# Band attention with split scores: the second score product over 128 contraction rows instead of 64

## The chip, the core and the metric

The kernel runs on one core of one Trainium2 chip. The metric is device time in microseconds (us) of one execution. Below, PE is the matrix engine (TensorE), PEld its weight loads, DVE the vector engine, ACT the scalar engine, POOL GpSimd and SP the engine that issues most DMAs.

## What is computed

One layer of a hybrid trunk on 1024 tokens of width 1024: a normalised input is projected once to q, k, v, gates and a state-space input; a band attention and a state-space mixer run on it; both are gated, merged, projected back, added to the input and normalised. Only the attention is touched here. It has 8 heads of 64 channels; a chunk of 64 queries sees its own chunk of keys and the 8 before it, with a bias by relative position:

```
scores = jnp.einsum("bnqhd,bnkhd->bnhqk", qc, k_band,
                    preferred_element_type=jnp.float32) * ATTN_SCALE
...
scores = jnp.where(valid, scores + bias[None, None], NEG_INF)
probs = jax.nn.softmax(scores, axis=-1).astype(v.dtype)
out = jnp.einsum("bnhqk,bnkhd->bnqhd", probs, v_band)
```

## The kernel before

**Split products.** Every matrix product is made from operands split in two parts: a high part rounded to the reduced type that PE reads (F32R), and a low part, the remainder. A projection adds three products into one PSUM bank (`mm3`, L104 to L106): high by high, high by low, low by high. The low by low part is left out.

**Scores.** A head has only 64 channels, so the 128 rows of the array are shared by two parts of a head. For head e of a pair, `qq` holds the high part of q twice (rows 0 to 63 and 64 to 127), `k2` holds the high part of k on the head's own rows (0 to 63 for the first head of a pair, 64 to 127 for the second) and the low part of k on the other rows. One product over 128 rows (L910) gives q high by k high plus q high by k low. The third term, q low by k high, is a second product over the 64 own rows only (L911); `ql` is one tile that holds the low q of both heads, each on its own rows. Both products accumulate into the same tile `s`.

**Where these come from.** `evac_q` (L690 to L704) runs once per half of the tokens and per pair of heads. It reads the projection's bank `mm` and for each head makes two ACT copies into `qq` (L702, the own rows; L703, the other rows) and one DVE subtraction into `ql` (L704; the trace records it under the helper's line L92). `evac_k` (L706) does the same for `k2`, with one ACT copy and one DVE subtraction per head.

**Order of the attention.** Heads are taken one after the other, query tiles of 128 in pairs. `scores` (L895) takes one query tile: with up to four key tiles it is one chunk of up to 512 columns, with five it is two chunks of 320. For each chunk PE runs L910 and L911, then DVE adds the bias and takes the row maximum (L912). ACT takes the exponential (L919), DVE a reciprocal (L920), POOL scales (L921). Two pairs of query tiles later (`LAG`), PE turns the probabilities (`turn`, L939), ACT and DVE split the turned tile into `th` and `tl` (L98, L101), and PE multiplies them with v (`prod`, L957 and L958) into `pv`, of which there is a single bank. When half of a head's queries is done, ACT and DVE add the two halves of `pv` to `y` (L964 and L965; DVE's part is recorded under L83), which frees that bank.

PE's order is written out by hand: `drive` interleaves the attention's steps with the pieces of projections (three products of 512 columns each): q and k of the next pair of heads during the first three pairs, gate columns during the last. The program's planner chooses the order on the other engines. Tile `s` has two PSUM banks (`ps_2`), the projections three (`ps_m`), the turned blocks two (`ps_t`).

The score products run from 244 to 472 us of the profile's span. The first pair's q is made before that stage, those of the other three pairs inside it.

Of the kernel before, what the change touches and what calls it, by code (L numbers as in the profile page):

```python
# [9 lines left out]
F32 = mybir.dt.float32  # L10
# [7 lines left out]
P = 128  # L18
L = 1024          # tokens
D = 1024          # model width  # L20
KT = D // P       # 8 k-tiles of the model width
HALF = 512
NH = 8
DH = 64
GC = 16           # channels of a state-space group
NS = 64           # states of a group
T8 = 8            # tokens of a state-space chunk
NJ = L // T8      # 128 chunks
NP = 16           # pairs of groups
MAGIC = 12582912.0  # L30
ET = mybir.EngineType
RATE_SSM = 1.0                              # steps of the state-space mixer per piece of a projection
SSM_STEPS = [8, 4, 4, 0, 2, 28, 20, 4]      # steps between its stages
RATE_ATT = 1.012                            # steps of the attention, relative to an even spread
PATTERN = "STSTT"                           # scores, and turns with products, in a step of the attention
LAG = 2                                     # pairs of query tiles between scores and products
NU = 4                                      # tiles of v from x * gain, scaled afterwards
NPM = 3                                     # psum banks of the projections
NPB = 7                                     # probability tiles
NGA = 5                                     # tiles of g_a during the third pair of heads  # L40
NWARM = 20
CUTS = [0, 512, 768, 1024]                  # column blocks of the last tile
# [3 lines left out]
def trunk_kernel(ctx: ExitStack, tc: tile.TileContext, x, x_t, ng, w_m, w_v, bias, a_re, a_im, log_dt,  # L46
# [26 lines left out]
    # the tensor engine's clock rises while the first loads are under way  # L73
# [34 lines left out]
    def rsqrt(pool_, v, out=None):  # L108
        """1 / sqrt(v), a few columns at a time: a root and a Newton step."""
        w = v.shape[1]  # L110
        r = pool_.tile([P, 4], F32, tag="rs_r", name="rs_r")[:, :w]
        u = pool_.tile([P, 4], F32, tag="rs_u", name="rs_u")[:, :w]
        vec.reciprocal(out=u, in_=v)
        last_sqrt[0] = act.activation(out=r, in_=u, func=AF.Sqrt)
        if w == 1:
            stt(u, r, v, r, MUL, MUL)
        else:
            tt(u, r, r, MUL)
            tt(u, u, v, MUL)
        ts(u, u, -0.5, MUL, 1.5, ADD)  # L120
        o = r if out is None else out
        tt(o, r, u, MUL)
        return o

    def rsqrt_mean(pool_, ss, n, eps, out=None):
        """1 / sqrt(ss / n + eps)"""
        v = pool_.tile([P, 4], F32, tag="rs_v", name="rs_v")[:, :ss.shape[1]]
        ts(v, ss, 1.0 / n, MUL, eps, ADD)
        return rsqrt(pool_, v, out)

# [1 line left out]
    # A task: (dma, split, run, number of yields of run). The weights of a task are loaded while  # L132
    # the one before it starts, and split into exact high and low parts in its middle.
# [14 lines left out]
    class Stream:  # L148
# [7 lines left out]
        def run(self, tasks, after=None):  # L156
            """Yields between pieces of the matrix products."""
            for n, (_, _, run, ny) in enumerate(tasks):
                nxt = tasks[n + 1] if n + 1 < len(tasks) else after
                w, raw = self.w, None  # L160
                if nxt is not None:
                    with tc.high_priority():
                        raw = nxt[0]()
                for i, _ in enumerate(run(w)):
                    if i == max(ny // 2 - 1, 0) and nxt is not None:
                        with tc.high_priority():
                            self.w = nxt[1](raw)
                    yield

    stream = Stream()  # L170
    hT = []           # [hi 0-3, hi 4-7], [lo 0-3, lo 4-7]

    def proj(w, half):
        """A projection tile: 128 columns of w_in on partitions, 512 tokens."""
        wh, wl = w
        ps = pm()
        sl = slice(half * HALF, (half + 1) * HALF)
        for k in range(KT):
            q, r = divmod(k, 4)
            mm3(ps, wh[:, k, :], wl[:, k, :], hT[0][q][:, r, sl], hT[1][q][:, r, sl], k == 0, k == KT - 1)  # L180
            if k < KT - 1:
                yield None
        yield ps

    def proj_task(src, evac):
        """evac(half, psum) takes the products of a half of the tokens."""
# [8 lines left out]
    def drive(main, back, rate):  # L195
        """Runs the generator main, and about rate steps of back for each of its steps."""
        acc = 0.0
        for _ in main:
            acc += rate() if callable(rate) else rate
            while acc >= 1.0:  # L200
                next(back, None)
                acc -= 1.0

# [1 line left out]
    sp = {}  # L205

    def ssm_params(tp, cpool):
# [63 lines left out]
        # cos and sin: quarter turns taken off exactly, then polynomials  # L271
# [38 lines left out]
        # powers of the discrete eigenvalue  # L310
# [9 lines left out]
        # B of the discrete system  # L320
# [18 lines left out]
        # |lambda|^8 and the unit phase to the 8th, then its powers of two  # L339
# [6 lines left out]
        def sqr(orr, oi, ar, ai):  # L346
# [4 lines left out]
            # the norm stays 1  # L351
# [13 lines left out]
        # D on the diagonal of the first tap  # L365
# [16 lines left out]
    def ssm_batch(b, sb, u_ready):  # L382
# [23 lines left out]
        # E: state at the end of a chunk from the chunk's inputs (rows: tap, channel)  # L406
# [6 lines left out]
        # Q: outputs from a state, by the age of the state (0..8)  # L413
# [40 lines left out]
        # powers of the chunk's phase  # L454
# [27 lines left out]
        # taps within a chunk, with D on the first, spread to a block Toeplitz matrix  # L482
# [34 lines left out]
    def load_x(i):  # L517
        """A tile of 128 tokens, for the mean squares."""
# [6 lines left out]
    def load_xt(i, whole=True):  # L525
        """The tile turned, for h^T."""
# [39 lines left out]
    def root(tiles):  # L566
        """One over the root mean square of each token."""
# [8 lines left out]
    def bcast(tiles):  # L576
        """The same on every partition."""
# [20 lines left out]
    def scale(i, q, bc):  # L598
        """h^T of a tile, a half of its rows."""
# [16 lines left out]
    def head(i, q):  # L616
        """x * gain, split."""
# [17 lines left out]
    def v_evac(ps, i):  # L635
        """The first tiles are products of x * gain, and take the mean squares here."""
# [19 lines left out]
    def u_task(b):  # L656
        box = {}

        def evac(half, ps):
# [3 lines left out]
            # the taps of a chunk in falling order  # L663
# [22 lines left out]
    def qk_tasks(p):  # L686
        """Heads 2p and 2p+1: [q;q] high, low q of both, [k high;k low] (second head: [low;high])."""
        hs = pairs[p] = [{}, {}]

        def evac_q(half, ps):  # L690
# [7 lines left out]
            sl = slice(half * HALF, (half + 1) * HALF)  # L698
            for e in range(2):
                own, oth = slice(64 * e, 64 * e + 64), slice(64 - 64 * e, 128 - 64 * e)  # L700
                qq, ql = hs[e]["qq"], hs[e]["ql"]
                act.activation(out=qq[own, sl], in_=ps[own], func=AF.Copy, scale=0.125)  # L702
                act.activation(out=qq[oth, sl], in_=ps[own], func=AF.Copy, scale=0.125)  # L703
                stt(ql[own, sl], ps[own], 0.125, qq[own, sl].bitcast(F32), MUL, SUB)  # L704
# [79 lines left out]
    def before(i, k):  # L784
        """What is emitted before product k of tile i."""
# [109 lines left out]
    def scores(h, i, bt, probs):  # L895
        """Exponentials of the scores of 128 queries, and one over their sums on a diagonal."""
        hd = pairs[h // 2][h % 2]
        e = h % 2
        own = slice(64 * e, 64 * e + 64)
# [7 lines left out]
        for c in range(nb):  # L907
# [3 lines left out]
            pe.matmul(ps, hd["ql"][own, qsl], hd["k2"][own, ksl], start=False, stop=True)  # L911
# [14 lines left out]
    class Values:  # L926
        """Probabilities turned, up to four blocks of 128 x 128 at a time, and multiplied by V."""
# [40 lines left out]
    # sigmoid(g_a) of the first tiles goes where the q and k of the pairs before were  # L968
# [19 lines left out]
    def turns(i):  # L988
        """The key tiles of the query tiles i and i + 1, in groups of at most four blocks."""
# [7 lines left out]
    def attention():  # L997
        """Pairs of query tiles; PATTERN: the order of scores, turns and products in a step."""
# [199 lines left out]
    with tc.tile_pool(name="fin", reuse_waits="tile", bufs=2) as fin:  # L1198
        fg_b = fin.tile([P, D], F32, name="fg_b", bufs=1)
        nc.scalar.dma_start(out=fg_b, in_=fg.partition_broadcast(P))  # L1200
        for i in range(KT):
# [13 lines left out]
            def add_x(n, ps):  # L1215
                """The row with x, its mean square so far, and the row times the gain."""
# [35 lines left out]
def _layout(inp):  # L1252
# [6 lines left out]
    wt = mt(w_in)                       # 40 tiles of 128 columns  # L1259
    # within a tile of the state-space channels: channel of a group first, then group  # L1260
# [4 lines left out]
             + list(range(24, 40)))     # u, z_a, q and k by head pairs, z_s, g_a, g_s  # L1265
# [48 lines left out]
```

## Time and profile before

| | |
|---|---|
| median of 3 runs | 837.65 us (837.37 to 838.12) |
| span of the profiled execution, first to last instruction | 836.3 us |
| PE busy over the span | 825.2 us (99%) |
| DVE busy | 480.9 us (58%) |
| ACT busy | 371.2 us (44%) |
| score products L910 and L911 | 96 each |

Of the profiled execution the page gives the span; the median of the runs is 1.35 us longer, which is what lies before the first and behind the last instruction, give or take the scatter of the runs.

How to read it: in a timeline row the first number is the start in us from the span's beginning, the second the duration. Matmuls are pipelined and the ends of their rows are modelled, so durations of neighbours overlap. What a matmul costs the stream is the distance from its start to the next start. PEld rows are weight loads: each matmul has one, and it can run beside the matmul before it. "idle before <-issue" on a PEld row is time in which the loading side stood still without any wait that the profile can name. `64*128` in a row is a weight tile of 64 rows.

### The profile page before, as it was taken

Reading aid. Unit: us, or ns where it says so; the run is one execution under the profiler, and the core shown is the slowest. Engines: PE = TensorE matmul, PEld = TensorE weight load, DVE = VectorE, ACT = ScalarE, POOL = GpSimd, SP = SyncE. Lnnn points to the kernel's source line nnn. Section 1 sums busy time; section 2 is a strip of 40 time slices with the busy share of each in tenths; the row PEclk is TensorE's granted clock in tenths of the full one; section 3 lists DMA queues with packets and bytes.
Section 4 is the critical chain, followed back from the end, with each engine's and each line's share of the span. In section 5 each row is a group of like instructions: output and inputs, shape, how many; then the busy total and the mean of one; then the engine's idle time right before and its main releaser. Section 6 shows DMA issues by size and latency. Waiting matters only on the chain.

```text
span 836.3 us, 11001 instructions
## 1 busy us (share of the span) xinstructions
PE 825.2 (99%) x3942; PEld 667.2 (80%) x3942; DVE 480.9 (58%) x1326; ACT 371.2 (44%) x701; POOL 127.2 (15%) x171
## 2 busy tenths in 40 slices
PE   8999999999999999999999999999999999999996
PEld 6878888888877777777777788888888888888885
DVE  6899898886646676676544532335353332354442
ACT  5652565645546456565443565116242211324332
POOL 4450022011003223323221200000000000001110
PEclk9999999999999999999999999999999999999999
DMA  8604352223330001110101044114113110042221
GB/s 310 246 26 125 91 137 69 100 81 119 112 107 31 23 31 42 42 42 1 42 26 51 26 141 136 62 41 150 51 51 114 41 62 13 6 145 101 101 101 51
DMA packets 32455, 67.84 MB, mean 81 GB/s; under 512 B 4560, under 2 KB 13776, under 8 KB 32400
## 3 DMA queue, kind: packets, MB, share of 16 engines
q1 hardware_dynamic: 27904, 61.35, 21.6%
q10 hardware_dynamic: 3344, 3.42, 1.4%
q0 software_dynamic: 1152, 2.36, 1.3%
q8 instruction: 31, 0.51, 0.2%
q14 instruction: 24, 0.20, 0.1%
HBM read 56.14 MB, written 10.98 MB: 80 GB/s over the span
## 4 chain that ended last, share of the span: by engine, by line
PE 96%; DVE 2%; DMA 1%; issue 0%; ACT 0%; SPq 0%; POOL 0%; ACTq 0%; POOLq 0%
PE mm L104 27%; PE mm L106 25%; PE mm L105 25%; PE s L911 4%; PE pt L939 3%; PE s L910 2%; PE pv L958 2%; PE pv L957 2%; PE pt L442 1%; PE b L468 1%; PE pt L503 1%; PE pt L504 1%; DMA xt<-in_x_t_dram 1%; DVE xt L601 0%; PE pt L426 0%
## 5 line engine op out<-in xcount | busy, mean ns | idle before, releaser
L104 PE MATMUL mm<-hT,w_hi 128*128 128x512 f32 x576 | 237.6, 413 | 0.0
L106 PE MATMUL mm<-hT,w_lo 128*128 128x512 f32 x576 | 225.7, 392 | 0.7 <-DVE w_lo L101 0.7
L105 PE MATMUL mm<-hT,w_hi 128*128 128x512 f32 x576 | 225.5, 392 | 0.0
L106 PEld LDWEIGHTS mm<-hT,w_lo 128*128 128x128 f32 x576 | 108.2, 188 | 24.3 <-DVE w_lo L101 1.2
L104 PEld LDWEIGHTS mm<-hT,w_hi 128*128 128x128 f32 x576 | 108.4, 188 | 23.2 <-issue 6.7
L105 PEld LDWEIGHTS mm<-hT,w_hi 128*128 128x128 f32 x576 | 108.7, 189 | 16.1 <-issue 0.4
L101 DVE TENSOR_TENSOR w_lo<-w_raw,w_hi 128x1024 fp32r<-128x1024 f32 x36 | 44.0, 1223 | 66.1 <-ACT w_hi L98 65.9
L912 DVE CUSTOM_DVE_ANT_0 p<-s,bias 128x320 f32<-128x320 f32 (+2 forms) x96 | 46.6, 490 | 34.0 <-PE s L911 31.7
L98 ACT ACTIVATE w_hi<-w_raw 128x1024 fp32r<-128x1024 f32 x36 | 38.1, 1059 | 62.9 <-PE mm L105 52.9
L101 DVE TENSOR_TENSOR tl<-pt,th 128x512 fp32r<-128x512 f32 (+2 forms) x72 | 43.2, 601 | 38.1 <-ACT th L98 37.6
L98 ACT ACTIVATE th<-pt 128x512 fp32r<-128x512 f32 (+2 forms) x72 | 37.8, 525 | 59.9 <-PE pt L939 54.0
L921 POOL TENSOR_SCALAR p<-p,sm 128x640 f32<-128x640 f32 (+2 forms) x64 | 42.5, 665 | 139.2 <-DVE sm L920 109.0
L919 ACT ACTIVATE p<-p,mx 128x640 f32<-128x640 f32 (+2 forms) x64 | 44.3, 692 | 38.3 <-DVE mx L89 18.2
L83 POOL TENSOR_TENSOR x<-x,fg_b 128x512 f32<-128x512 f32 (+1 forms) x9 | 11.0, 1225 | 319.0 <-ACT o L1219 319.0
L104 PE MATMUL mm<-y_hi,o_hi 128*128 128x512 f32 x128 | 49.8, 389 | 0.0
L105 PE MATMUL mm<-y_lo,o_hi 128*128 128x512 f32 x128 | 49.8, 389 | 0.0
L106 PE MATMUL mm<-y_hi,o_lo 128*128 128x512 f32 x128 | 49.8, 389 | 0.0
L98 ACT ACTIVATE o_hi<-o_raw 128x512 fp32r<-128x512 f32 x24 | 15.0, 631 | 71.7 <-PE mm L105 60.3
L911 PE MATMUL s<-k,ql 64*128 64x320 f32 (+2 forms) x96 | 39.3, 409 | 0.0
L939 PE MATMUL pt<-ident,p 128*128 128x128 f32 x240 | 38.9, 276 | 0.0
L957 PE MATMUL pv<-th,vt 128*128 128x256 f32 x144 | 36.0, 272 | 0.2
L939 PEld LDWEIGHTS pt<-ident,p 128*128 128x128 f32 x240 | 28.9, 140 | 9.0 <-issue 1.9
(231 smaller groups left out, 1512.8 us busy)
## 6 DMA issues: line engine op xcount, KB each, us to landing
w_raw<-in_w_m_dram SPq DMA_DIRECT2D x36, 512.0 KB, 3.3
x<-in_x_dram SPq DMA_DIRECT2D x16, 512.0 KB, 6.3
wo_raw<-in_w_out_dram SPq DMA_DIRECT2D x8, 512.0 KB, 3.2
xt<-in_x_t_dram SPq DMA_DIRECT2D x6, 512.0 KB, 9.7
bias<-in_bias_dram SPq DMA_DIRECT2D x8, 320.0 KB, 2.8
wv_raw<-in_w_v_dram SPq DMA_DIRECT2D x8, 256.0 KB, 5.6
u_dr<-us SPq DMA_DIRECT2D x4, 512.0 KB, 3.6
uu<-u_dr SPq DMA_DIRECT2D x4, 512.0 KB, 3.8
```

Of the source, the lines that this page charges most:

```text
L98: act.activation(out=hi, in_=src, func=AF.Copy)
L101: (eng or vec).tensor_tensor(out=lo, in0=src, in1=hi.bitcast(F32), op=SUB)
L104: pe.matmul(ps, lh, rh, start=first, stop=False)
L105: pe.matmul(ps, lh, rl, start=False, stop=False)
L106: pe.matmul(ps, ll, rh, start=False, stop=last)
L910: pe.matmul(ps, hd["qq"][:, qsl], hd["k2"][:, ksl], start=True, stop=False)
L911: pe.matmul(ps, hd["ql"][own, qsl], hd["k2"][own, ksl], start=False, stop=True)
L912: vec.tensor_tensor_reduce(out=pr[:, c * cw:(c + 1) * cw], in0=ps, in1=bt[:, 640 - w + c * cw:640 - w + (c + 1) * cw], scale=1.0, scalar=- ...
L919: act.activation(out=pr[:, :w], in_=pr[:, :w], func=AF.Exp, bias=mx[:, 0:1], accum_out=sm)
L921: pool.tensor_scalar(out=pr[:, :w], in0=pr[:, :w], scalar1=sm, scalar2=1.0, op0=MUL, op1=MUL)
L939: last_turn[0] = pe.transpose(tp[:, n:n + P], probs[h, q][:, k * P:(k + 1) * P], ident).ins
L957: pe.matmul(o, lhs, th[:, cs], start=first and n == 0, stop=False)
```

## The change

Two edits.

In `scores`, the second product runs over all 128 rows of `ql` and `k2`. On the own rows it gives low q by high k as before. On the other rows it now multiplies the other head's low q by this head's low k, which is not wanted.

In `evac_q`, that extra term is taken off in advance: the copy of `qq` on the other rows, which meets the low k in the first product, is no longer the high part of q but q (scaled) minus the other head's low q. What is added in the second product cancels in the first. The ACT copy L703 becomes a DVE operation of the same shape, and it has to wait for the other head's `ql`.

```
     def evac_q(half, ps):
...
             sl = slice(half * HALF, (half + 1) * HALF)
+            own = [slice(64 * e, 64 * e + 64) for e in range(2)]
+            ql = hs[0]["ql"]
             for e in range(2):
-                own, oth = slice(64 * e, 64 * e + 64), slice(64 - 64 * e, 128 - 64 * e)
-                qq, ql = hs[e]["qq"], hs[e]["ql"]
-                act.activation(out=qq[own, sl], in_=ps[own], func=AF.Copy, scale=0.125)
-                act.activation(out=qq[oth, sl], in_=ps[own], func=AF.Copy, scale=0.125)
-                stt(ql[own, sl], ps[own], 0.125, qq[own, sl].bitcast(F32), MUL, SUB)
+                qq = hs[e]["qq"]
+                act.activation(out=qq[own[e], sl], in_=ps[own[e]], func=AF.Copy, scale=0.125)
+                stt(ql[own[e], sl], ps[own[e]], 0.125, qq[own[e], sl].bitcast(F32), MUL, SUB)
+            for e in range(2):
+                oth = own[1 - e]
+                stt(hs[e]["qq"][oth, sl], ps[own[e]], 0.125, ql[oth, sl].bitcast(F32), MUL, SUB)
...
     def scores(h, i, bt, probs):
         hd = pairs[h // 2][h % 2]
-        e = h % 2
-        own = slice(64 * e, 64 * e + 64)
...
             pe.matmul(ps, hd["qq"][:, qsl], hd["k2"][:, ksl], start=True, stop=False)
-            pe.matmul(ps, hd["ql"][own, qsl], hd["k2"][own, ksl], start=False, stop=True)
+            pe.matmul(ps, hd["ql"][:, qsl], hd["k2"][:, ksl], start=False, stop=True)
```

The rest of the diff removes comments. Numbers and order of the instructions on PE stay the same.

## The prediction

> **What bounds the kernel now.** I read the page first: busy times, then the chain that ended last.
>
> ```profile
> span 836.3 us, 11001 instructions
> ...
> PE 825.2 (99%) x3942; PEld 667.2 (80%) x3942; DVE 480.9 (58%) x1326; ACT 371.2 (44%) x701; POOL 127.2 (15%) x171
> ...
> PE 96%; DVE 2%; DMA 1%; issue 0%; ACT 0%; SPq 0%; POOL 0%; ACTq 0%; POOLq 0%
> ```
>
> The matrix engine is the bound nearly everywhere: what is taken from PE's stream comes off the end, as long as nobody else becomes late. But "busy" only says that a matmul was under way. So next the busy time by stretches, for the stage of the score products and for what follows it. The columns are the stretch, its length, the busy time (and instructions) of PE, PEld, DVE, ACT and POOL, the granted clock, the DMA share and GB/s:
>
> ```profile
> 244.00:472.00 228.00, 227.76 (x1139) 170.78 (x1137) 140.57 (x430) 124.36 (x261) 61.32 (x89) 1.00 0.10 33
> 472.00:836.00 364.00, 356.96 (x1623) 296.88 (x1622) 143.96 (x273) 120.89 (x231) 14.41 (x12) 1.00 0.24 80
> ```
>
> In the 228 us of the stage PE has 0.2 us without a matmul, DVE is at 62%, ACT at 55%, and the clock is full. Third, the view of the tile `s`, whose row for L911 gives the number of second products and their widths (the 8 that are missing from its list are 512 wide):
>
> ```profile
> L911 PE MATMUL s<-k,ql x96: 323/410/502, 244.5 to 472.0; 64*128 64x320 f32 x64, 64*128 64x128 f32 x8, 64*128 64x256 f32 x8, 64*128 64x384 f32 x8
> ```
>
> Fourth, PE's timeline, in which I read distances from start to start. A tile with one chunk of 512 columns, then the three products of a projection:
>
> ```profile
> 302.34 0.45 PE L910 MATMUL s<-k,qq 128*128 128x512 f32 x1
> 302.71 0.49 PE L911 MATMUL s<-k,ql 64*128 64x512 f32 x1
> 303.14 0.50 PE L104 MATMUL mm<-hT,w_hi 128*128 128x512 f32 x1
> 303.48 0.40 PE L105 MATMUL mm<-hT,w_hi 128*128 128x512 f32 x1
> 303.71 0.39 PE L106 MATMUL mm<-hT,w_lo 128*128 128x512 f32 x1
> ```
>
> All five stream 512 columns. L105 to L106, full rows behind full rows, takes 0.23 us. L911 takes 0.43, L910 ahead of it 0.37, and L104 behind it 0.34. So the short product costs more than a full one, and its neighbours on both sides pay too. The weight loads of the same moment show why:
>
> ```profile
> 302.71 0.18 PEld L911 LDWEIGHTS s<-k,ql 64*128 64x128 f32 x1 [0.24 <-issue]
> 303.14 0.19 PEld L104 LDWEIGHTS mm<-hT,w_hi 128*128 128x128 f32 x1 [0.24 <-issue]
> 303.24 0.19 PEld L105 LDWEIGHTS mm<-hT,w_hi 128*128 128x128 f32 x1
> ```
>
> The load for L105 starts at 303.24, while L104 (from 303.14) runs, and is hidden. The loads into 64 rows, and the first into 128 rows behind them, start only when their own matmul does, after 0.24 us in which the loading side stood still with no wait named. Each change between 128 and 64 rows stops the stream; there are two for each of the 96 chunks.
>
> **What the change removes on PE.** With all rows used there is no change of rows, and I price each score product as a full-row matmul of its width. A tile of five key tiles (two chunks of 320), with a 256-column product ahead of it:
>
> ```profile
> 306.82 0.28 PE L958 MATMUL pv<-tl,vt 128*128 128x256 f32 x1
> 306.93 0.31 PE L910 MATMUL s<-k,qq 128*128 128x320 f32 x1
> 307.17 0.41 PE L911 MATMUL s<-k,ql 64*128 64x320 f32 x1
> 307.51 0.41 PE L910 MATMUL s<-k,qq 128*128 128x320 f32 x1
> 307.85 0.41 PE L911 MATMUL s<-k,ql 64*128 64x320 f32 x1
> 308.19 0.50 PE L104 MATMUL mm<-hT,w_hi 128*128 128x512 f32 x1
> 308.53 0.40 PE L105 MATMUL mm<-hT,w_hi 128*128 128x512 f32 x1
> ```
>
> Now the four products take 308.19 - 306.93 = 1.26 us. A full-row matmul takes 0.11 for 256 columns (306.82 to 306.93) and 0.23 for 512; 320 columns lie a quarter of the way between, about 0.145 (an estimate from these two). Four make 0.58, so a tile saves 0.68. 64 chunks are 32 tiles: 32 x 0.68 = 21.8 us.
>
> The narrowest chunk, and the pair of 128-column products to price it by:
>
> ```profile
> 346.68 0.22 PE L910 MATMUL s<-k,qq 128*128 128x128 f32 x1
> 346.83 0.33 PE L911 MATMUL s<-k,ql 64*128 64x128 f32 x1
> 347.09 0.66 PE L939 MATMUL pt<-ident,p 128*128 128x128 f32 x4
> ...
> 348.53 0.22 PE L957 MATMUL pv<-th,vt 128*128 128x128 f32 x1
> 348.59 0.27 PE L958 MATMUL pv<-tl,vt 128*128 128x128 f32 x1
> 348.69 0.45 PE L104 MATMUL mm<-hT,w_hi 128*128 128x512 f32 x1
> ```
>
> 347.09 - 346.68 = 0.41 becomes 0.16: 0.25 saved, eight times, 2.0 us. The 512-wide chunk above takes 0.80 and becomes 2 x 0.23 = 0.46: 0.34 saved, eight times, 2.7 us. For the sixteen chunks of 256 and 384 I take 0.30 each, between those two: 4.8 us.
>
> Then the matmul behind each tile. L104 behind an L911 takes 0.34 (308.19 to 308.53, and 303.14 to 303.48) and would take 0.23: 0.11 saved. I count 45 of the 64 tiles with an L104 behind them in this timeline (the two above are two of them): 5.0 us. Behind the others come transposes, for which I take nothing.
>
> Sum on PE: 21.8 + 2.0 + 2.7 + 4.8 + 5.0 = 36.3 us.
>
> A rule that speaks against this: in the Trainium skill, "TensorE: Matmul & The Clock Gate", Part 3, under what overlaps and what doesn't, loads are said to overlap running matmuls only when their row groups differ. By it, a full-row load behind a full-row matmul would stay exposed and the 36.3 us would be near zero; the load of L105 above, hidden under L104 in the same rows, contradicts it here.
>
> **What the change adds.** In `evac_q` the ACT copy L703 turns into a DVE operation that reads `mm` and `ql`. Its nearest rows, from the views of the lines L92 and L703:
>
> ```profile
> L92 DVE SCALAR_TENSOR_TENSOR ql<-mm,qq x16: 675/689/697, 225.7 to 376.4; 64x512 fp32r<-64x512 f32 x16
> L703 ACT ACTIVATE qq<-mm x16: 588/592/597, 225.0 to 375.6; 64x512 fp32r<-64x512 f32 x16
> ```
>
> ACT loses 16 x 0.59 us, which is off the path. DVE gains 16 x 0.69 us of the same shape. Four of the sixteen belong to the first pair, from 225.7 us on, before any score; the other twelve, 8.3 us, fall into the stage. DVE's busy time there goes from 140.6 to 148.9 us, in 228 - 36.3 = 191.7 us: 78%. The work fits, but DVE takes its instructions in order, and each q half puts two of these, 1.4 us, in a stretch that is already tight. Behind them in DVE's queue stand the next `tl`, the bias additions (L912) and `y`; PE waits for each of those. At one place it already does:
>
> ```profile
> 376.37 0.69 DVE L92 SCALAR_TENSOR_TENSOR ql<-mm,qq 64x512 fp32r<-64x512 f32 x1
> 377.10 0.15 DVE L87 TENSOR_SCALAR mx<-mx 128x1 f32<-128x1 f32 x1
> 377.28 0.68 DVE L83 TENSOR_TENSOR y<-pv,y 64x512 f32<-64x512 f32 x1
> ```
>
> ```profile
> 377.50 0.40 PE L106 MATMUL mm<-hT,w_lo 128*128 128x512 f32 x1
> 378.02 0.38 PE L957 MATMUL pv<-th,vt 128*128 128x256 f32 x1
> ```
>
> `y` ends at 377.96 and the next product into the one bank `pv` starts at 378.02, 0.52 us after L106 instead of 0.23: PE lost 0.3 us. Two more operations ahead of `y` would add up to 1.4 us, less the 0.6 us by which the last `ql` comes earlier because ACT's queue has a copy less ahead of it. So the price of the added work on the path lies between 0 (it goes into DVE's idle time) and 8.3 us (all of it exposed). I take the middle, 4.1 us: I assume that half of the q halves end with `y` behind them in the queue, as here, and that the others find gaps. A price below zero, from the time that ACT gains, I exclude since no PE row above waits for ACT alone.
>
> **A second cost: DVE's pace behind the chunks.** Tile `s` has two banks, so a chunk's L910 waits for L912 of the chunk before the last.
>
> ```profile
> 338.18 0.49 DVE L912 CUSTOM_DVE_ANT_0 p<-s,bias 128x320 f32<-128x320 f32 x1
> ```
>
> ```profile
> 338.86 0.49 DVE L912 CUSTOM_DVE_ANT_0 p<-s,bias 128x320 f32<-128x320 f32 x1 [0.18 <-PE s L911]
> ```
>
> ```profile
> 340.14 0.41 PE L910 MATMUL s<-k,qq 128*128 128x320 f32 x1
> ```
>
> Two chunks are 0.68 us apart on DVE, exactly as far as PE now makes them (307.85 - 307.17). After the change PE makes one in 0.29. At this place L912 ends at 339.35 and the L910 that needs its bank starts at 340.14: 0.79 us of slack. PE would come 0.39 us earlier (0.11 at L104, 0.095 at the L910 behind a product of full rows, 0.195 at one L911), and DVE's second L912 would end 0.39 us later against its matmul: the slack is just gone. I take 1 us over the stage, with ends at 0 and at 0.3 us for each of the 32 two-chunk tiles, 9.6 us, about what DVE's excess pace costs where the slack starts smaller.
>
> **The sum.** 836.3 - 36.3 + 4.1 + 1.0 = 805.1 us of span. The median of the runs lies 1.35 us above the span, so 806.5 us.
>
> **The rivals.**
>
> A. DVE becomes the pace of the stage. All of the added work and all of the chunk waits come through: 8.3 + 9.6 = 17.9 us are given back, 837.65 - 36.3 + 17.9 = 819.3 us. For it: 78% busy with in-order waits, and the tight place at 376 us. Against: DVE's rows are short, and 43 us of the stage remain idle on it. 0.15.
>
> B. The stop is not a matter of rows: two products of the scores stay 0.34 apart also with full rows, because the load isn't hidden or because they add into one bank. Then PE gains nothing and DVE's work is paid: 837.65 + 4.1 = 841.8 us, from 837.65 to 846 by the ends above. This ends slower. It decides if an L911 of 320 columns starts 0.29 us or more after its L910: then about a quarter of the gain is left, near what DVE may cost. Against it: L104 to L106 add into one bank too, in full rows, at 0.23 us, with hidden loads. 0.03.
>
> C. The clock: full rows switch twice as many cells, and the granted clock could fall. The stage would need about 228 - 31 = 197 us at full clock, so it ends slower than now below 197 / 228 = 0.86. At 0.81 it would take 243 us, 853 us in all. Against it: from 472 us on PE runs full rows for 357 of 364 us at a clock of 1.00, in the row above. 0.02.
>
> **How the numbers follow.** My forecast, the gain with a few us given back, has 0.80. Its own bounds are 837.65 - 36.3 = 801.4 (nothing given back) and about 813; with half a us more on either term of PE and with A up to nearly its full price the range is 800 to 818. It leaves out the rest of A, B and C. The three runs lie within 0.1%, so a change of 0.2%, 1.7 us, can be told from none. Faster: forecast and A, 0.95. Same: B where DVE's work is hidden, 0.01. Slower: the rest of B, and C, 0.04.
>
> **What would show it right or wrong.** In the changed profile, L911 of 320 columns should stand about 0.145 us behind its L910, and L104 behind a tile take 0.23 us; the "issue" idle time ahead of L911's loads should vanish. The stage should last about 197 us, with PE idle for some 5 us in it, put down to DVE (`y`, `tl`, or L912), mostly where a q half ends. If L911 still costs 0.3 us, B is true and the step on hidden loads is wrong. If PE stands idle for 15 us or more behind DVE, A is true. If the stage is short by 36 us, the DVE terms were paid by idle time. A clock below 1.00 in the stage means C.

## The result

| | before | changed |
|---|---|---|
| median of 4 runs, us | 837.88 (837.37 to 838.95) | 806.50 (806.0 to 807.3) |
| ratio, 95% interval | | 0.9626 (0.9612 to 0.9640) |
| span of the profiled execution, us | 836.3 | 804.5 |
| first score product to the L104 behind the last one, us | 244.37 to 472.29: 227.92 | 243.99 to 441.27: 197.28 |

The change takes 31.4 us off. In the profiled executions it is 31.8 us, of which 30.64 lie between the first score product and the matmul behind the last one. I call that stretch the stage. Its length is the number to compare below, since it leaves out what the loads at the start of the kernel scatter. Lines have moved by four: L914 and L915 are the score products, L916 the bias addition, L943 the transposes, L961 and L962 the products with v.

The page of the changed kernel, its span, its busy times and its chain:

```profile
span 804.5 us, 11004 instructions
...
PE 791.9 (98%) x3942; PEld 663.6 (82%) x3942; DVE 487.9 (61%) x1342; ACT 361.1 (45%) x685; POOL 128.6 (16%) x171
...
PE 89%; DVE 7%; ACT 2%; issue 1%; DMA 1%; POOL 0%; ACTq 0%; DVEq 0%
```

PE still sets the end, but DVE has gone from 2% to 7% of the chain. The stage by itself, in the busy times by stretches:

```profile
243.99:441.27 197.28, 194.91 (x1138) 167.29 (x1136) 143.18 (x442) 116.25 (x249) 61.44 (x89) 1.00 0.12 38
```

The clock column is 1.00, as before. PE's time without a matmul is 2.4 us here (197.28 - 194.91), where it was 0.2. Then PE's timeline, a tile of two chunks:

```profile
302.94 0.31 PE L914 MATMUL s<-k,qq 128*128 128x320 f32 x1
303.08 0.31 PE L915 MATMUL s<-k,ql 128*128 128x320 f32 x1
303.23 0.31 PE L914 MATMUL s<-k,qq 128*128 128x320 f32 x1
303.38 0.31 PE L915 MATMUL s<-k,ql 128*128 128x320 f32 x1
303.52 0.60 PE L943 MATMUL pt<-ident,p 128*128 128x128 f32 x4
```

The four products take 303.52 - 302.94 = 0.58 us; they took 1.26. Their weight loads, from the loading side's timeline, start one matmul ahead, and no "issue" time stands before them:

```profile
302.94 0.19 PEld L915 LDWEIGHTS s<-k,ql 128*128 128x128 f32 x1
303.12 0.19 PEld L914 LDWEIGHTS s<-k,qq 128*128 128x128 f32 x1
303.23 0.19 PEld L915 LDWEIGHTS s<-k,ql 128*128 128x128 f32 x1
```

Where PE now stands still is seen at two kinds of places. The first is a chunk that waits for a bank of `s`, which DVE has not yet read (PE's timeline; the bracket is the idle time and what ended it):

```profile
248.47 0.31 PE L914 MATMUL s<-k,qq 128*128 128x320 f32 x1
248.62 0.31 PE L915 MATMUL s<-k,ql 128*128 128x320 f32 x1
249.54 0.38 PE L914 MATMUL s<-k,qq 128*128 128x320 f32 x1 [0.61 <-DVE sm L924]
```

L915 should be followed after 0.145 us and is followed after 0.92. The second is where q is evacuated for the second half of the tokens. PE:

```profile
312.26 0.40 PE L106 MATMUL mm<-hT,w_lo 128*128 128x512 f32 x1
312.71 0.38 PE L961 MATMUL pv<-th,vt 128*128 128x256 f32 x1
...
314.21 0.28 PE L961 MATMUL pv<-th,vt 128*128 128x256 f32 x1
314.98 0.39 PE L962 MATMUL pv<-tl,vt 128*128 128x256 f32 x1 [0.50 <-DVE tl L101]
```

and DVE at the same time:

```profile
310.90 0.69 DVE L92 SCALAR_TENSOR_TENSOR ql<-mm,qq 64x512 fp32r<-64x512 f32 x1
...
311.98 0.68 DVE L83 TENSOR_TENSOR y<-pv,y 64x512 f32<-64x512 f32 x1
...
312.75 1.39 DVE L92 SCALAR_TENSOR_TENSOR qq<-mm,ql 64x512 fp32r<-64x512 f32 x2
...
314.24 1.02 DVE L101 TENSOR_TENSOR tl<-pt,th 128x512 fp32r<-128x512 f32 x2
```

The two new operations (1.39 us) run behind `y`, not ahead of it. What they delay is the next `tl`, and PE's product L962 waits for that: 0.77 us from L961 to L962 instead of 0.12.

To size all of this I took, for every matmul of the stage, the distance to the next start less the median distance of its kind (same line, width and neighbouring lines), and summed what exceeds 0.04 us. These stops are 5.5 us longer than before: 5.5 us given back. The stream itself thus lost 30.64 + 5.5 = 36.1 us. This is an estimate: with wider or narrower kinds the 5.5 becomes 4.1 to 5.1, and the 36.1 becomes 34.7 to 35.7.

### The profile page after: what moved, and what is told of

Read it like the earlier page. It is cut to its first block, busy times and chain, and to the rows that moved or that the text cites. A ratio compares the mean times of both kernels' runs of the same rounds, so it can differ in the third digit from the quotient of the medians.

```text
span 804.5 us, 11004 instructions
## 1 busy us (share of the span) xinstructions
PE 791.9 (98%) x3942; PEld 663.6 (82%) x3942; DVE 487.9 (61%) x1342; ACT 361.1 (45%) x685; POOL 128.6 (16%) x171
## 4 chain that ended last, share of the span: by engine, by line
PE 89%; DVE 7%; ACT 2%; issue 1%; DMA 1%; POOL 0%; ACTq 0%; DVEq 0%
PE mm L104 25%; PE mm L106 25%; PE mm L105 25%; PE pt L943 2%; PE pv L962 2%; PE s L914 1%; PE pv L961 1%; DVE p L916 1%; PE s L915 1%; DVE tl L101 1%; PE pt L442 1%; PE b L468 1%; PE pt L503 1%; PE pt L504 1%; DVE qq L92 1%
## 5 line engine op out<-in xcount | busy, mean ns | idle before, releaser
L104 PE MATMUL mm<-hT,w_hi 128*128 128x512 f32 x576 | 233.1, 405 | 0.0
L106 PE MATMUL mm<-hT,w_lo 128*128 128x512 f32 x576 | 225.6, 392 | 0.8 <-DVE w_lo L101 0.8
L105 PE MATMUL mm<-hT,w_hi 128*128 128x512 f32 x576 | 225.4, 391 | 0.0
L106 PEld LDWEIGHTS mm<-hT,w_lo 128*128 128x128 f32 x576 | 108.1, 188 | 24.4 <-DVE w_lo L101 1.2
L105 PEld LDWEIGHTS mm<-hT,w_hi 128*128 128x128 f32 x576 | 108.6, 189 | 16.4 <-issue 0.4
L104 PEld LDWEIGHTS mm<-hT,w_hi 128*128 128x128 f32 x576 | 108.4, 188 | 16.2 <-issue 0.2
L916 DVE CUSTOM_DVE_ANT_0 p<-s,bias 128x320 f32<-128x320 f32 (+2 forms) x96 | 44.2, 485 | 17.1 <-PE s L915 16.6
L106 PE MATMUL mm<-y_hi,o_lo 128*128 128x512 f32 x128 | 49.8, 389 | 0.0
L104 PE MATMUL mm<-y_hi,o_hi 128*128 128x512 f32 x128 | 49.8, 389 | 0.0
L105 PE MATMUL mm<-y_lo,o_hi 128*128 128x512 f32 x128 | 49.8, 389 | 0.0
L943 PE MATMUL pt<-ident,p 128*128 128x128 f32 x240 | 38.1, 273 | 0.0
L962 PE MATMUL pv<-tl,vt 128*128 128x256 f32 x144 | 36.3, 281 | 1.0 <-DVE tl L101 1.0
L83 DVE TENSOR_TENSOR x<-mm,x 128x512 f32<-128x512 f32 (+1 forms) x17 | 11.2, 660 | 41.5 <-PE mm L106 41.5
L961 PE MATMUL pv<-th,vt 128*128 128x256 f32 x144 | 36.2, 272 | 0.2
```

Source lines behind the costliest of these rows:

```text
L83: (eng or vec).tensor_tensor(out=o, in0=a, in1=b, op=op)
L104: pe.matmul(ps, lh, rh, start=first, stop=False)
L105: pe.matmul(ps, lh, rl, start=False, stop=False)
L106: pe.matmul(ps, ll, rh, start=False, stop=last)
L916: vec.tensor_tensor_reduce(out=pr[:, c * cw:(c + 1) * cw], in0=ps, in1=bt[:, 640 - w + c * cw:640 - w + (c + 1) * cw], scale=1.0, scalar=- ...
L943: last_turn[0] = pe.transpose(tp[:, n:n + P], probs[h, q][:, k * P:(k + 1) * P], ident).ins
```

## The experiments

Theory 1 is what this trace suggests: the price is paid at each change between 128 and 64 rows; of the 5.5 us given back some 3 are waits for the two banks of `s`, and some 1.5 the added DVE work. Theory 2 keeps the split of the prediction: 4.1 us for the added work and 1.0 for the banks. The score stage in each kernel, from PE's timeline, and the times (the kernel before was timed beside each group, with medians of 839.06, 839.57 and 838.13 us):

| run | time, us | ratio to before (95%) | stage, us |
|---|---|---|---|
| before | 837.88 | | 244.37 to 472.29: 227.92 |
| changed | 806.50 | 0.9626 (0.9612 to 0.9640) | 243.99 to 441.27: 197.28 |
| e1_no_correction | 808.27 | 0.9637 (0.9624 to 0.9650) | 245.66 to 442.21: 196.55 |
| e2_evac_only | 838.79 | 1.0003 (0.9993 to 1.0014) | 244.93 to 473.64: 228.71 |
| e3_grouped | 828.39 | 0.9874 (0.9855 to 0.9893) | 246.09 to 463.41: 217.32 |
| e5_evac_twice | 814.59 | 0.9711 (0.9693 to 0.9730) | 245.07 to 448.73: 203.66 |
| after_again | 808.83 | 0.9634 (0.9616 to 0.9651) | 244.28 to 441.69: 197.41 |
| e6_three_s_banks | 818.64 | 0.9758 (0.9743 to 0.9774) | 257.33 to 452.69: 195.36 |
| e7_two_pv_banks | 821.77 | 0.9792 (0.9777 to 0.9807) | 257.30 to 454.29: 196.99 |
| e8_before_three_banks | 851.67 | 1.0147 (1.0130 to 1.0164) | 256.77 to 484.69: 227.92 |
| after_third | 806.50 | 0.9622 (0.9603 to 0.9641) | 244.05 to 441.33: 197.28 |
| e9_lent_bank | 804.99 | 0.9602 (0.9585 to 0.9619) | 244.70 to 440.01: 195.31 |
| e10_lent_bank_y_first | 804.66 | 0.9599 (0.9581 to 0.9616) | 246.27 to 441.64: 195.37 |

The stage of the changed kernel came out at 197.28, 197.41 and 197.28 us in its three profiles, so a difference of half a us in this column means something.

### Full rows without the correction

```
                 act.activation(out=qq[own[e], sl], in_=ps[own[e]], func=AF.Copy, scale=0.125)
+                act.activation(out=qq[own[1 - e], sl], in_=ps[own[e]], func=AF.Copy, scale=0.125)
                 stt(ql[own[e], sl], ps[own[e]], 0.125, qq[own[e], sl].bitcast(F32), MUL, SUB)
-            for e in range(2):
-                oth = own[1 - e]
-                stt(hs[e]["qq"][oth, sl], ps[own[e]], 0.125, ql[oth, sl].bitcast(F32), MUL, SUB)
```

> Full rows in the second product, but the other rows of qq are the plain high copy by ACT as before; the other head's term is left in, so the scores carry a small extra term. The 12 added DVE operations of the stage are gone. Theory 1 (the added DVE work costs about 1.5 us on the path, the rest of the 5.5 us given back is the wait for the two banks of s): 804.5 to 805.5 us. Theory 2 (the split of the prediction: 4.1 us for the added work, 1.0 for the banks): 802.4 us. If the full-row products were not the cause of the gain, about 838.

Taking the 12 DVE operations away shortens the stage by 0.73 us only, and the time of the whole does not fall at all (the intervals of the two ratios overlap). Theory 2, with 802.4 us, is out; theory 1 put their price too high as well. PE's timeline shows what came in their place, and the rows of DVE below it show what stands ahead of `y`:

```profile
313.66 0.40 PE L106 MATMUL mm<-hT,w_lo 128*128 128x512 f32 x1
314.63 0.39 PE L959 MATMUL pv<-th,vt 128*128 128x256 f32 x1 [0.57 <-DVE y L83]
```

```profile
312.43 0.41 DVE L914 CUSTOM_DVE_ANT_0 p<-s,bias 128x256 f32<-128x256 f32 x1
...
312.98 0.69 DVE L92 SCALAR_TENSOR_TENSOR ql<-mm,qq 64x512 fp32r<-64x512 f32 x1
...
313.89 0.68 DVE L83 TENSOR_TENSOR y<-pv,y 64x512 f32<-64x512 f32 x1
```

The product into `pv` now waits for `y` (0.97 us after L106; in the changed kernel 312.71 - 312.26 = 0.45). DVE's order is that of the kernel before: a bias addition (L914) stands ahead of the second `ql`, and `y` behind both. In the changed kernel `ql` comes first (310.90, the addition at 311.62), and `y` starts 0.28 us ahead of L106 (311.98), not 0.23 behind it. So the new `evac_q` removed a wait at this place, too, and the 0.73 us are a net price. ACT makes its second copies of q again here, but its half of `y` has ended at 313.42, before DVE starts its own; whether the copies delay `ql` or only the planner's order does was not separated.

### The correction without full rows

```
+        own = slice(64 * (h % 2), 64 * (h % 2) + 64)
...
-            pe.matmul(ps, hd["ql"][:, qsl], hd["k2"][:, ksl], start=False, stop=True)
+            pe.matmul(ps, hd["ql"][own, qsl], hd["k2"][own, ksl], start=False, stop=True)
```

> The new evac_q alone; the second product stays on 64 rows, so the correction is taken off but never added back. Theory 1: the 12 operations of 0.69 us hide in DVE's idle time of the slower stage, 837.9 to 839. Theory 2: 4 us, 842. PE's distances in the score products as in the kernel before (0.34 us).

The stage is 0.79 us longer than in the kernel before, and the ratio is 1.0003 (0.9993 to 1.0014). This is the same price from the other side: the new `evac_q` costs 0.7 to 0.8 us of the stage, whether PE is fast or slow in the scores.

The four kernels also give the gain of the full rows alone. DVE and ACT run the same order of instructions in e1_no_correction as in the kernel before, and in e2_evac_only as in the changed kernel; each pair differs only in the rows of the second product. The stage falls by 227.92 - 196.55 = 31.4 us in one pair and by 228.71 - 197.28 = 31.4 us in the other.

### Two changes of rows per tile instead of four

```
+        for ps, ksl in zip(pss, ksls):
+            pe.matmul(ps, hd["qq"][:, qsl], hd["k2"][:, ksl], start=True, stop=False)
+        for ps, ksl in zip(pss, ksls):
+            pe.matmul(ps, hd["ql"][own, qsl], hd["k2"][own, ksl], start=False, stop=True)
```

> The kernel before, but in the 32 tiles of two chunks both L910 come first and then both 64-row products, so a tile changes rows twice and not four times. Theory 1 (the price is paid at each change of rows): a tile with the L104 behind it goes from 1.60 to 0.145 + 0.24 + 0.145 + 0.34 + 0.34 = 1.21 us, 12.5 us in all, 825.4 us. Rival (every 64-row product is slow by itself, 0.34 us, and delays the one behind): 0.145 + 0.24 + 0.34 + 0.34 + 0.34 = 1.41, 6.2 us in all, 831.7 us.

PE's timeline of a tile, with neighbours of one kind merged (x2), and the loads of the short products:

```profile
334.97 0.45 PE L910 MATMUL s<-k,qq 128*128 128x320 f32 x2
335.36 0.56 PE L912 MATMUL s<-k,ql 64*128 64x320 f32 x2
335.84 0.50 PE L104 MATMUL mm<-hT,w_hi 128*128 128x512 f32 x1
336.18 0.39 PE L105 MATMUL mm<-hT,w_hi 128*128 128x512 f32 x1
```

```profile
335.35 0.29 PEld L912 LDWEIGHTS s<-k,ql 64*128 64x128 f32 x2 [0.19 <-issue]
```

From the first L910 to L105 it is 336.18 - 334.97 = 1.21 us, the 1.21 of theory 1 and not the 1.41 of its rival. The second of the two short products has this row of its own:

```profile
335.61 0.31 PE L912 MATMUL s<-k,ql 64*128 64x320 f32 x1
```

So the first short product is followed after 0.25 us and the second, behind which the rows change back, after 0.23; neither takes the 0.34 of a short product between full ones. The sum of theory 1 came out, but not its split of these two (0.145 and 0.34). The load of the second is hidden (0.29 us for two loads of 0.18). The price lies in the change of rows: the tile with its L104 falls from 1.60 to 1.21 us for two changes less, about 0.2 us for each. The rows put about half of it ahead of the change and half behind: against the 0.145 of a full product, the L910 ahead of the first change takes 0.24 and the short product behind it 0.25; the short product ahead of the second change takes 0.23, and the L104 behind it 0.34 instead of 0.23. The Trainium skill says in "TensorEngine Tiling (Array Packing)", section Key Properties, that changing the tiling mode drains the engine; the distances here agree with that and give it a price. Of the 12.5 us expected, the stage kept 10.6 (227.92 - 217.32). The rest was given back; the next tile has the load of its second L910 held for 0.17 us by DVE, but the 1.9 us were not taken apart.

### The added DVE work twice

```
             for e in range(2):
                 oth = own[1 - e]
                 stt(hs[e]["qq"][oth, sl], ps[own[e]], 0.125, ql[oth, sl].bitcast(F32), MUL, SUB)
+            for e in range(2):
+                oth = own[1 - e]
+                stt(hs[e]["qq"][oth, sl], ps[own[e]], 0.125, ql[oth, sl].bitcast(F32), MUL, SUB)
```

> The changed kernel with both new DVE operations of evac_q written twice (the same values again): 12 more operations of 0.69 us in the stage, 8.3 us of DVE work. Theory 1 (most of it hides): 1.5 to 3 us more, 808 to 809.5 us. Theory 2 (half of it is exposed): 4.1 us or more, 810.6 us and up.

Both theories were too low: the stage grows by 6.4 us, from 197.28 to 203.66, for 8.3 us of DVE work. The first 8.3 us, which came in place of ACT copies, cost 0.7 net; the second cost 6.4. The waits of PE in the stage (columns: who waited for whom, us in total, times, longest) name the places:

```profile
PE s L917 <- DVE mx L919: 3.7, 8, 0.7
PE pv L964 <- DVE mx L87: 3.1, 2, 1.6
```

The doubled operations hold up the bias additions and with them the banks of `s`, and `y` with the bank of `pv`: the two chains of the prediction. But the second helping does not only meet fuller gaps, it also comes in another order. DVE at the place shown above:

```profile
315.63 1.41 DVE L92 SCALAR_TENSOR_TENSOR qq<-mm,ql 64x512 fp32r<-64x512 f32 x2
317.07 0.68 DVE L83 TENSOR_TENSOR y<-pv,y 64x512 f32<-64x512 f32 x1
...
318.44 1.41 DVE L92 SCALAR_TENSOR_TENSOR qq<-mm,ql 64x512 fp32r<-64x512 f32 x2
```

One pair of the operations now stands ahead of `y`, where in the changed kernel both stood behind it; the same happens near 364 us, and the two waits behind `y` (3.1 us) are at these two places. So the run shows that more work at these places is dear in the order that the planner chose. That the gaps take one helping and no more is not shown.

### Where the rest was given back: the banks

The changed kernel with three banks for `s` instead of two, and two for the projections instead of three:

```
-NPM = 3
+NPM = 2
```

> The changed kernel once more, on the chip of the three below, so that they are compared with it and not only with the kernel before: ratio 0.963 to the kernel before, score stage 197.3 us.

> The changed kernel with three PSUM banks for s and two for the projections (instead of two and three). Theory 1, by the stops in the trace of the changed kernel: 3.1 us of PE's waits are for a bank of s, so the score stage falls from 197.3 to about 194.3 us, unless two banks are too few for the projections. Theory 2 (the banks of s cost 1 us): 196.3 us. No change at all would mean that DVE's own pace and not the number of banks sets these waits.

The stage falls by 2.05 us (197.41 to 195.36), between the two theories and nearer to the first. But the whole is 10 us slower by the medians (13 us in the profiled executions), since the stage begins 13 us later: ahead of it the projections need their third bank. The control shows both halves of this:

> Control: the kernel before with three banks of s and two of the projections. In it no wait for a bank of s was found, so the stage should stay at 227.9 us; anything longer is the price of the missing projection bank, inside the stage or elsewhere in the kernel.

In the kernel before, the third bank of `s` changes the stage by nothing, 227.92 us both times; the 12 us are lost ahead of the stage (it starts at 256.77 instead of 244.37). So the wait for a bank of `s` is not an old wait; it came with the faster products.

Two banks for `pv` instead:

```
-NPM = 3
+NPM = 2
...
-    ps_2 = ctx.enter_context(tc.tile_pool(name="ps_2", bufs=5 - NPM, space=PSUM))
+    ps_2 = ctx.enter_context(tc.tile_pool(name="ps_2", bufs=2, space=PSUM))
...
-    ps_v = ctx.enter_context(tc.tile_pool(name="ps_v", bufs=1, space=PSUM))
+    ps_v = ctx.enter_context(tc.tile_pool(name="ps_v", bufs=2, space=PSUM))
```

> The changed kernel with two banks for pv, two for s, two for the projections. Theory 1: only the waits of pv behind y go, 0.9 us in all, stage 196.4 us; the next wait for tl at the same two places stays. Rival (the single bank of pv is what holds PE where a q half ends): 2.5 us less, 194.8 us.

0.4 us less in the stage. The waits behind `y` are gone, but the wait for `tl` two products later grows by about 0.3 us at each of the two places. The single bank of `pv` is not what holds PE there; DVE's queue is.

### A bank lent for the stage

```
+    ps_x = ctx.enter_context(tc.tile_pool(name="ps_x", bufs=1, space=PSUM))
...
+    def s_bank():
+        turn_s[0] += 1
+        if turn_s[0] % 3 == 0:
+            return ps_x.tile([P, HALF], F32, tag="x", name="s")
+        return ps_2.tile([P, HALF], F32, tag="s", name="s")
...
-            ps = ps_2.tile([P, HALF], F32, tag="s", name="s")[:, :cw]
+            ps = s_bank()[:, :cw]
```

Outside the stage the projections use that bank as their third, as before.

> The changed kernel on the chip of the two below: ratio 0.963, stage 197.3 us.

> The changed kernel in which the projections lend their third bank to s during the score stage only. If two banks of the projections are only too few before and after the stage, the 2 us that three banks of s saved in the stage are kept and the 13 us lost ahead of it are not: stage 195.4 us, 2 us less than the changed kernel. If the lent bank collides at the ends of the stage, nothing is gained.

The stage falls to 195.31 us, 1.97 less than the changed kernel on the same chip, and nothing is lost ahead of it. The place shown above, where the third chunk waited 0.61 us, now reads:

```profile
248.74 0.31 PE L927 MATMUL s<-k,qq 128*128 128x320 f32 x1
248.89 0.31 PE L928 MATMUL s<-k,ql 128*128 128x320 f32 x1
249.03 0.30 PE L927 MATMUL s<-k,qq 128*128 128x320 f32 x1
```

Why it is 2 us, and not the 3.1 us to which the stops for a bank of `s` add up in the changed kernel, is seen in the list of PE's waits around the stage, in the columns used above:

```profile
PE pt L956 <- POOL p L938: 1.1, 1, 1.1
PE pv L975 <- DVE tl L114: 1.0, 2, 0.5
```

The list names no wait for `s` any more, but a new one: right behind the place above, a transpose (L956) waits 1.1 us for the probabilities `p` that POOL scales. The list of e6_three_s_banks has the same wait. So part of what the third bank frees is lost one step further down the same chain: scores, maximum, exponential, scaling, transpose. DVE's order differs in places from that of the changed kernel in both runs, so the bank and the order were not separated.

804.99 us is below both kernels, with a ratio of 0.9602 to the kernel before; against the changed kernel's 0.9622 the intervals overlap, so the gain of some 2 us rests on the stage.

And the same with `y` ahead in the planner's order:

```
-                last_act[0] = act.copy(out=y[own], in_=po[64:128]).ins
-                tt(y[own], po[0:64], y[own], ADD)
+                with tc.high_priority():
+                    last_act[0] = act.copy(out=y[own], in_=po[64:128]).ins
+                    tt(y[own], po[0:64], y[own], ADD)
```

> The same, with the ACT copy and the DVE addition of y ahead of the q evacuation in the planner's order. Theory 1: the two places where pv waits for y and then for tl (1.1 us each) get shorter; stage 194 us. Rival: the wait moves to the bank of the projection or to tl, no change against the lent bank alone.

Nothing changed (195.37 us): the stops of 0.2 us for `y` and 0.65 for `tl` are still at the same two places. But neither did the order: PE, DVE, ACT and POOL run their instructions in the order of e9_lent_bank, and `y` stood ahead of the two new operations there already (311.52 and 312.30; here 313.16 and 313.94). So this is a second measurement of the lent bank. It decides nothing between theory 1 and the rival.

## Why the prediction was right

**The bound and the gain on PE: right, by their own working.** The forecast was 36.3 us off the stream; it was 36.1 by the stops. The terms can also be added up from the median distances of the two profiles: 21.5 us for the 320-column tiles, 1.9 for the narrowest chunks, 2.5 for the 512-column ones (by those that no stop disturbs), 4.5 for those of 256 and 384, and 4.8 for the 45 L104 come to 35.2. The transposes behind the other 19 tiles, for which the prediction took nothing, gave 1.1 us more: the first of them takes 0.11 us instead of 0.165. Each price held: 0.145 us for 320 columns, 0.58 for a tile, no unexplained "issue" time before the loads. The L104 behind a score product takes 0.23 us again, as in this pair of rows of the changed kernel:

```profile
246.18 0.39 PE L104 MATMUL mm<-hT,w_hi 128*128 128x512 f32 x1
246.41 0.40 PE L105 MATMUL mm<-hT,w_hi 128*128 128x512 f32 x1
```

The two pairs of kernels with one and the same `evac_q` show that the full rows alone take 31.4 us off the stage. The grouped kernel shows that the cause was the change of rows and not the short product itself, which the prediction had only argued from the loads.

**The sum given back: right in size, wrong in its parts.** 5.1 us were forecast, 5.5 came. The first term, 4.1 us for the added DVE work on the path, was mis-sized: the new `evac_q` costs 0.7 to 0.8 us net, by taking the work away and by adding it alone. Two of its steps failed. At the two places where `pv` waits for `y` (near 312 and 358 us) it assumed that the new operations stand ahead of `y` in DVE's queue; the planner put them behind it. And it excluded any gain from the new `evac_q`; but with the old one the wait for `y` at these places is longer (`pv` starts 0.97 us behind L106 instead of 0.45), and what the new one adds there is the wait for `tl`. The second term, 1.0 us for the banks of `s`, was mis-sized the other way: PE's stops for them add up to 3.1 us, of which a third bank takes back 2.0 net, with a wait of 1.1 us for POOL new in their place. The two errors nearly cancelled, which is luck and not method. Some 2.8 us of the 5.5 (5.5 - 0.7 - 2.0) were not taken away by any run; the stops for `y` and `tl` that are left at the ends of the q halves, and the wait for POOL, are part of them.

**The rivals.** A, DVE as the pace of the stage, did not come: DVE was busy for 143.18 of 197.28 us, 73% and not 78%. With twice the added work 6.4 of the next 8.3 us came through, in part behind `y`, ahead of which the planner had put a pair of the operations. B fell with the first score product, 0.14 us behind its neighbour. C: the granted clock is 1.00 in the stage.

## What to carry to other kernels

Read distances between starts, not durations, and compare a short matmul with its neighbours: a product over fewer rows between full ones can cost more than a full one, because of the two changes. If the rows cannot be filled, put products of equal rows together; that alone gave a third of the gain here. Before adding work to an engine that is three quarters busy, ask what stands behind it in the queue at the very place where it lands: 8.3 us of work, behind `y` where `y` was urgent, cost 0.7 us net; another 8.3 us, with which a part of it came ahead of `y`, cost 6.4. And when a run is to test an order, look first whether the order changed.

## What the runs showed of the hardware that was not expected

A change between 128-row and 64-row matmuls costs about 0.2 us at 320 columns, whichever way, about half on the matmul ahead of it and half on the one behind, and 64-row loads behind a 64-row matmul on the same rows are hidden like full ones (two of them in 0.29 us). The prediction had the price only for the two changes of a chunk together, and could not tell what a short product costs among its like.
